# A two-layer encoder on one core: the last norm's scale row made on chip instead of through DRAM, and its finishing products placed wider apart

## The chip, the cores and the metric

The kernel runs on one core of one Trainium2 chip. The metric is the device time of one execution in microseconds (us). Three runs of the kernel before took 3623.66, 3624.28 and 3625.88 us; their median is 3624.28 us.

## The reference

The reference is an encoder trunk of two layers over 2048 tokens of 1024 features, in float32. Layer 0 mixes tokens by windowed attention, layer 1 by latent attention. Behind each mixer a gated input embedding is added, and behind the last layer stands one more norm. Only this ending matters here:

```python
for i in range(DEPTH):
    ...
    h = h + y
    gate = jax.nn.sigmoid(rms_norm(h, ple_norm_g[i]) @ ple_w_gate[i])
    h = h + (p[i] @ ple_w[i]) * gate
return rms_norm(h, final_norm_g)

def rms_norm(x, g):
    xf = x.astype(jnp.float32)
    y = xf * lax.rsqrt(jnp.mean(xf * xf, axis=-1, keepdims=True) + EPS)
    return (y * g.astype(jnp.float32)).astype(x.dtype)
```

So the last norm needs, for every token, one over the root of the mean square of its 1024 features, and it can be computed only when all 1024 features of `h` for that token are there.

## The kernel before

Activations lie in SBUF with features on the 128 partitions and tokens along the free dimension, so 1024 features are eight tiles, f = 0 to 7, and a reduction over features is a matmul with a matrix of ones. Each float32 product is made from three matmuls of split operands (`mm3`, L294 to L296), so one output tile of 128 features x 512 tokens takes 8 x 3 = 24 matmuls. Below, these 24 are called a product.

The end of the program is the second `Post` object (layer 1, `self.final`). Its back half goes over five token groups, `self.segs`: groups 0, 1 and 2 of 512 tokens, groups 3 and 4 of 256. For each group and each f:

- PE makes the gate product (`back`).
- `mixin` runs through the other engines: DVE takes the product out of PSUM and scales it (L926), ACT applies the sigmoid (L931), POOL multiplies by the embedding tile (L933), DVE adds to the residual `hf` (L935), ACT squares the new `hf` (L831).
- `gather` adds the square to the group's accumulator (L837, on POOL; for group 4 on DVE).
- The embedding tile comes from DRAM by `p_load` (L908, issued by SP) into a ring of two tiles, so load f + 2 can be issued only when POOL has used tile f.
- During groups 0 to 2 ACT and DVE also split the residual of a later group into matmul operands (`h_cut`, L232 and L233). The residual tiles of groups 3 and 4 are loaded (L891) into the same SBUF tiles that group 0 leaves free.

When all eight squares of a group are gathered, the scale row (1 / rms, for every token, on all 128 partitions) has to be made, and then `finish` (L944, DVE) multiplies each of the eight `hf` tiles by gain and row, and `h_store` (L940, SP) writes it out. There are two ways to the row:

- Groups 0 to 2 use `sums_at`: split the accumulator (ACT L220, DVE L222), two matmuls with ones (L270), copy one row to SBUF (L849), write it to DRAM (`sum_out`, L860), read it back with tokens on partitions (L866), take the root (L240, ACT L244, L248 to L253), write it to DRAM again (`root_out`, L880) and read it back spread over all partitions (`row_in`, L287).
- Groups 3 and 4 use `turn`, six steps on chip: one float32 matmul of ones with the accumulator (L954), DVE picks the diagonal of each 128 x 128 piece into a column (L960), root as above, PE transposes the broadcast column back (L974), ACT copies the row to SBUF (L978).

The order of the work on PE, DVE, ACT and POOL is written out by hand. `Plan.add(t, f, ...)` records a step with a planned time, the steps are sorted by it, and each engine runs its instructions strictly in that order. The times have meaning only for the order. One product is `UNIT` = 5.19 of them. The order of DMAs on SP is not set by the plan; a scheduler of the framework sets it, and SP too runs in order, so a DMA that waits holds up all behind it. `PS_SB` = 10 and `SUMS` place the steps of `sums_at` behind a group's end, `PL_SUM` those of `turn` for group 3.

Of the kernel before, what the change touches and what calls it, by code (L numbers as in the profile page):

```python
# [21 lines left out]
NC8 = D // P  # L22
TG = 512
# [12 lines left out]
PS_X, PS_EV, PS_ST, PS_SS, PS_H, PS_P, PS_HS, PS_SB = 4.4, 0.61, 2.06, 9.3, 1.2, 3, 0.68, 10  # L36
# [14 lines left out]
SUMS = (3, 4.2, 5, 7.5, 16.5, 16.7, 19, 20)  # L51
CUTAT, GATHB = (2.7, 1.9), 7.05
G_W, G_U = (-15.79, -9, 2, 8), -9.81
PL_SUM = (4.5, 5.8, 6.6, 8, 9.5, 10.6)
VLAG, GATHAT, ACCAT, DENAT, RECIPAT = 4.3, 1.3, 1.4, 8.4, 13.4
KLAG, RLAG, OLAG, DLAG, ILAG = 1, 0.8, 1, 0.8, 0.6
KAT = (6, 12)
# [78 lines left out]
class Plan:  # L136
# [5 lines left out]
    def add(self, t, f, *args):  # L142
        self.steps.append((t, f, args))
# [537 lines left out]
class Post:  # L681
# [329 lines left out]
    def schedule(self, plan, base, tables):  # L1011

        add = lambda t, f, *args: plan.add(base + t * US, f, *args)
        for t, f, args in tables:
            add(t, getattr(self, f), *args)
        add(5 if self.final else 0.3, self.spread_init)
        for tg in range(NG):
            for f in range(NC8):
                t = (NC8 * tg + f) * UNIT
                te = t + UNIT + PS_EV  # L1020
                add(t, self.front, tg, f)
                add(te - PS_X, self.x_load, tg, f)
                add(te, self.add, tg, f)
                add(te + 0.9, self.x_square, tg, f)
                add(te + 1.6, self.gather, 1, tg, f)
                add(te + PS_ST, self.x_store, tg, f)
                if tg > 0:
                    before = 3 + f // 2 if tg == 1 else NC8 * (tg - 1) + f
                    to = (3 + f / 2 if tg == 1 else before) * UNIT + 0.6
                    add(to - PS_OL2 - (6 if tg > 1 else 1.3), self.o_load, tg, f)  # L1030
                    add(before * UNIT - 0.01, self.o_spread, tg, f)
                    add(to, self.o_gate, tg, f, "both")
                    add(to + CUTAT[tg > 1], self.o_cut, tg, f, "both")
                    if f == 0:
                        add(to - 9, self.spread_load, tg)
                        add(to - 4.5, self.spread_cut, tg)
            self.sums_at(add, NC8 * (tg + 1) * UNIT + (PS_SS if tg < NG - 1 else 6.29), 1, tg)
        t = NG * NC8 * UNIT
        for tg in range(NG):
            tb = t + NC8 * tg * UNIT  # L1040
            add(tb - (PS_R1 if tg < NG - 1 else PS_R2), self.row_in, 1, tg)
            for f in range(NC8):
                th = tb - NC8 * UNIT + (0.5 + 0.8 * f if tg == 0 else 1.2 + 0.75 * f) * UNIT + PS_H
                add(th - PS_HL - (0 if tg == 0 else 2), self.h_load, tg, f)
                add(th, self.h_cut, tg, f)
        for g, (lo, n) in enumerate(self.segs):
            x, last = n / TG, self.final and g == len(self.segs) - 1
            unit = x * UNIT
            for f in range(NC8):
                te = t + unit + PS_EV  # L1050
                add(t, self.back, g, f)
                add(te - PS_P, self.p_load, g, f)
                for i, dt in enumerate((0, 0.9, 1.7, 3.2, 4.1) if n == TG else (0, 0.55, 1, 1.9, 2.5)):
                    add(te + dt, self.mixin, g, f, i)
                if last or g == len(self.segs) - 1 and f == NC8 - 1:
                    dt = 4.9 if n == TG else 3
                else:
                    dt = GATHB if n == TG else 3.7
                add(te + dt, self.gather, 2, g, f, "vector" if last else "gpsimd")
                t += unit  # L1060
                if not self.final:
                    add(te + 4.2 + PS_HS, self.h_store, g, f)
            if not self.final or n == TG:
                self.sums_at(add, t + (PS_SB if n * (g + 1) < T else PS_SL), 2, g)
            else:
                if last:
                    add(te + 0.6, self.warm_root)
                    for f in (2, 5):
                        add(te + 2.7, self.gain, g, f)
                times = [te + 3.1 + 0.01 * i for i in range(6)] if last else [te + dt for dt in PL_SUM]  # L1070
                for i in range(6):
                    add(times[i], self.turn, g, i)
                for f in range(NC8):
                    if last:
                        add(times[5] + 0.01 + 0.01 * f, self.finish_last, g, f)
                    else:
                        add(times[5] + 0.8 + f, self.finish, g, f)
                        add(times[5] + 1.6 + f, self.h_store, g, f)
            if self.final and n == TG:
                fin = t + PS_SB + 26  # L1080
                add(fin - 3, self.row_in, 2, g)
                for f in range(NC8):
                    add(fin + 1.3 * x * f, self.finish, g, f)
                    add(fin + 1.3 * x * f + 1, self.h_store, g, f)

    def enter(self, plan, base, early):

# [753 lines left out]
```

## Time and profile before

| | |
|---|---|
| median of three runs | 3624.28 us |
| the profiled execution | 3625.45 us |
| its span, first to last instruction | 3623.7 us |
| PE busy in the span | 3522.8 us (97%) |
| DVE, ACT, POOL busy | 2453.7, 2277.4, 1987.7 us |
| mean granted TensorE clock | 0.990 of 2.4 GHz |

The profiled execution is 1.75 us longer than its span, and 1.17 us longer than the median of the runs. All times of rows below are microseconds from the start of the span. A row of the timeline gives start, duration, engine, line, operation, and in brackets the idle time of the engine before it and what ended that.

### The profile page before, as it was taken

Reading aid. Unit: us, or ns where it says so; the run is one execution under the profiler, and the core shown is the slowest. Engines: PE = TensorE matmul, PEld = TensorE weight load, DVE = VectorE, ACT = ScalarE, POOL = GpSimd, SP = SyncE. Lnnn points to the kernel's source line nnn. Section 1 sums busy time; section 2 is a strip of 40 time slices with the busy share of each in tenths; the row PEclk is TensorE's granted clock in tenths of the full one; section 3 lists DMA queues with packets and bytes.
Section 4 is the critical chain, followed back from the end, with each engine's and each line's share of the span. In section 5 each row is a group of like instructions: output and inputs, shape, how many; then the busy total and the mean of one; then the engine's idle time right before and its main releaser. Section 6 shows DMA issues by size and latency. Waiting matters only on the chain.

```text
span 3623.7 us, 52443 instructions
## 1 busy us (share of the span) xinstructions
PE 3522.8 (97%) x17118; PEld 2949.7 (81%) x17118; DVE 2453.7 (68%) x4539; ACT 2277.4 (63%) x4268; POOL 1987.7 (55%) x1565
## 2 busy tenths in 40 slices
PE   7999999999999899999999999999999999989996
PEld 6888878877888889898888888888888888868876
DVE  6111169997456544425989898989898989985465
ACT  6211179995244533423889898989898989952332
POOL 5331210024334422113889898989898989964343
PEclk9999999999999999999999999999999999999998
DMA  5332388887655865834121212121212121066533
GB/s 187 136 122 90 94 208 202 201 201 225 190 147 150 195 223 185 267 122 107 43 54 42 52 31 53 33 58 36 59 35 57 34 68 36 20 195 205 164 96 105
DMA packets 380098, 428.19 MB, mean 118 GB/s; under 512 B 46303, under 2 KB 233183, under 8 KB 379118
## 3 DMA queue, kind: packets, MB, share of 16 engines
q1 hardware_dynamic: 360814, 390.75, 39.0%
q10 hardware_dynamic: 19008, 34.09, 2.5%
q8 instruction: 134, 2.20, 0.3%
q14 instruction: 142, 1.16, 0.1%
HBM read 251.65 MB, written 156.17 MB: 113 GB/s over the span
## 4 chain that ended last, share of the span: by engine, by line
PE 84%; DVE 6%; DMA 3%; ACT 2%; issue 2%; POOL 1%; SPq 0%; ACTq 0%; DVEq 0%; POOLq 0%
PE ps L296 13%; PE ps L294 13%; PE ps L295 13%; PE ps L1620 7%; PE ps L1653 6%; PE ps L1651 6%; PE ps L1683 6%; PE ps L1652 6%; PE ps L1684 6%; PE ps L601 2%; PE ps L615 1%; DVE blkF L935 1%; PE ps L557 1%; PE ps L556 1%; PE ps L616 1%
## 5 line engine op out<-in xcount | busy, mean ns | idle before, releaser
L1663 POOL TENSOR_TENSOR blkR<-blkF,blkX 128x512 fp32r<-128x512 f32 x1024 | 1352.0, 1332 | 179.3 <-PE ps L1653 51.7
L1624 DVE TENSOR_REDUCE blkF<-ps 128x1 f32<-128x512 f32 x1024 | 700.3, 684 | 79.4 <-PE ps L1620 43.7
L1655 ACT ACTIVATE blkF<-ps 128x512 f32<-128x512 f32 x1024 | 611.5, 597 | 100.6 <-PE ps L1653 57.2
L1656 ACT CAST blkX<-blkF 128x512 fp32r<-128x512 f32 x1024 | 635.5, 621 | 32.8
L1673 DVE TENSOR_TENSOR ps<-ps,blkF 128x512 f32<-128x512 f32 x896 | 615.3, 687 | 0.7
L1684 PE MATMUL ps<-blkR 128*128 128x512 f32 x1024 | 405.7, 396 | 1.1 <-POOL blkR L1663 1.1
L1683 PE MATMUL ps<-blkX,blkR 128*128 128x512 f32 x1024 | 405.7, 396 | 0.0
L294 PE MATMUL ps<-blkR 128*128 128x512 f32 (+2 forms) x888 | 337.7, 380 | 3.2 <-ACT blkR L220 2.8
L296 PE MATMUL ps<-blkR 128*128 128x512 f32 (+2 forms) x888 | 336.0, 378 | 0.5 <-DVE blkR L222 0.5
L295 PE MATMUL ps<-blkR 128*128 128x512 f32 (+2 forms) x888 | 335.6, 378 | 0.0
L367 DVE TENSOR_TENSOR blkF<-ps,blkF 128x512 f32<-128x512 f32 x72 | 49.5, 691 | 301.8 <-PE ps L296 292.1
L222 POOL TENSOR_TENSOR blkR<-blkF,blkR 128x512 fp32r<-128x512 f32 (+1 forms) x40 | 74.0, 1855 | 302.2 <-ACT blkR L220 274.9
L831 ACT ACTIVATE blkF<-blkF 128x512 f32<-128x512 f32 (+1 forms) x120 | 72.4, 603 | 261.2 <-DVE blkF L935 139.0
L1684 PEld LDWEIGHTS ps<-blkR 128*128 128x128 f32 x1024 | 195.0, 190 | 46.9 <-POOL blkR L1663 2.3
L1683 PEld LDWEIGHTS ps<-blkX,blkR 128*128 128x128 f32 x1024 | 195.0, 190 | 44.3
L837 POOL TENSOR_TENSOR blkF<-blkF 128x512 f32<-128x512 f32 (+1 forms) x112 | 159.5, 1424 | 99.3 <-ACT blkF L831 98.3
L933 POOL TENSOR_TENSOR blkF<-blkF 128x512 f32<-128x512 f32 (+1 forms) x70 | 85.8, 1225 | 223.2 <-ACT blkF L931 192.5
L294 PEld LDWEIGHTS ps<-blkR 128*128 128x128 f32 x888 | 168.0, 189 | 34.5 <-ACT blkR L220 3.1
L296 PEld LDWEIGHTS ps<-blkR 128*128 128x128 f32 x888 | 167.6, 189 | 31.6 <-DVE blkR L222 1.2
L295 PEld LDWEIGHTS ps<-blkR 128*128 128x128 f32 x888 | 167.9, 189 | 28.2
L227 DVE TENSOR_TENSOR blkR<-ps,blkR 128x512 fp32r<-128x512 f32 (+2 forms) x232 | 143.6, 625 | 47.5 <-ACT blkR L226 47.3
L1651 PE MATMUL ps<-blkZ 96*128 96x512 f32 x384 | 155.6, 405 | 6.8 <-ACT blkF L1655 6.8
(272 smaller groups left out, 9110.2 us busy)
## 6 DMA issues: line engine op xcount, KB each, us to landing
h<-blkF SPq DMA_DIRECT2D x96, 256.0 KB
blkF<-h SPq DMA_DIRECT2D x82, 256.0 KB
a_qs<-blkF ACTq DMA_DIRECT2D x64, 256.0 KB
ple<-blkF SPq DMA_DIRECT2D x64, 256.0 KB
b_v<-blkX SPq DMA_DIRECT2D x32, 512.0 KB
b_q<-blkX SPq DMA_DIRECT2D x64, 256.0 KB
blkZ<-b_q SPq DMA_DIRECT2D x64, 256.0 KB
blkF<-h SPq DMA_DIRECT2D x31, 512.0 KB
```

The lines of the kernel that those rows point to most:

```text
L294: mm(out, lhsT=lh, rhs=rh, start=(first and i == 0), stop=False)
L295: mm(out, lhsT=lh, rhs=rl, start=False, stop=False)
L296: mm(out, lhsT=ll, rhs=rh, start=False, stop=(last and i == n - 1))
L1620: nc.tensor.matmul(ps, lhsT=qh[0:96, qt * P : (qt + 1) * P], rhs=self.kh[h % 3][0:96, kc * TG : (kc + 1) * TG], start=True, stop=True,)
L1624: nc.vector.tensor_reduce(out=mm[:, qt, kc : kc + 1], in_=ps, axis=AX.X, op=ALU.max)
L1651: nc.tensor.matmul(sp, lhsT=kl[:, kt_], rhs=qh[0:96, :], start=True, stop=False)
L1655: nc.scalar.activation(pe, sp, AF.Exp, scale=SCALE_B)
L1656: nc.scalar.copy(ph, pe)
L1663: nc.gpsimd.tensor_tensor(out=pl, in0=pe, in1=fv(ph), op=ALU.subtract)
L1673: nc.vector.tensor_tensor(out=st["acc"], in0=prev, in1=st[kt][0], op=ALU.add)
L1683: nc.tensor.matmul(st["o"], lhsT=v, rhs=ph, start=(kt == 0), stop=False)
L1684: nc.tensor.matmul(st["o"], lhsT=v, rhs=pl, start=False, stop=(kt == NT - 1))
```

## The change

Groups 0 to 2 make their row by `turn` like groups 3 and 4, with planned times `PT_TURN` behind the group's end; nothing of them goes by DRAM any more. `sums_at` and `row_in` for the last norm are gone. The eight `finish` steps of a full group follow the row at a distance of 2.3 each, where it was 1.3, and they start at about 22.6 behind the group's end (19.9 for group 2), where it was 36. `PL_SUM` of group 3 is later by 2.3 to 2.8, and its `finish` steps are 0.85 apart, where it was 1. In the changed kernel all lines of the functions concerned have numbers larger by one.

```diff
-PL_SUM = (4.5, 5.8, 6.6, 8, 9.5, 10.6)
+PL_SUM = (7.1, 8.4, 8.9, 11, 12.3, 13)
+PT_TURN = ((10.37, 11.8, 12.4, 14.5, 20.75, 21.6), (10.37, 11.8, 12.4, 14.5, 18.15, 18.9))
...
-            if not self.final or n == TG:
+            if not self.final:
                 self.sums_at(add, t + (PS_SB if n * (g + 1) < T else PS_SL), 2, g)
+            elif n == TG:
+                times = PT_TURN[g == 2]
+                for i, dt in enumerate(times):
+                    add(t + dt, self.turn, g, i)
+                for f in range(NC8):
+                    add(t + times[5] + 1 + 2.3 * f, self.finish, g, f)
+                    add(t + times[5] + 2 + 2.3 * f, self.h_store, g, f)
...
-                        add(times[5] + 0.8 + f, self.finish, g, f)
-                        add(times[5] + 1.6 + f, self.h_store, g, f)
-            if self.final and n == TG:
-                fin = t + PS_SB + 26
-                add(fin - 3, self.row_in, 2, g)
-                for f in range(NC8):
-                    add(fin + 1.3 * x * f, self.finish, g, f)
-                    add(fin + 1.3 * x * f + 1, self.h_store, g, f)
+                        add(times[5] + 0.8 + 0.85 * f, self.finish, g, f)
+                        add(times[5] + 1.6 + 0.85 * f, self.h_store, g, f)
```

On PE the two matmuls of L270 stood behind the third product of the next group (the sixth, for the half products of group 3). Now one float32 matmul of 512 columns stands behind the second (the fourth) product, and four transposes stand behind the fourth (the seventh). The matmul for group 3's row moves from behind the second product of group 4 to behind the third.

On SP, this is the stretch of groups 3 and 4 in the kernel before, where group 2's row goes out and comes back (`rs`); `ple` rows are the embedding loads, `out` rows the stores.

```order
L908 DMA blkF<-ple_84 128x256
L866 DMA blkF<-sq_92 128x4x1
L908 DMA blkF<-ple_84 128x256 x4
L880 DMA rs_97<-blkF 128x4x1
L287 DMA blkF<-rs_97 128x512
L908 DMA blkF<-ple_84 128x256
L940 DMA out<-blkF 128x256
```

The same stretch on SP in the changed kernel:

```order
L909 DMA blkF<-ple_84 128x256 x9
L941 DMA out<-blkZ 128x512 x2
L909 DMA blkF<-ple_84 128x256
L941 DMA out<-blkZ 128x512
L909 DMA blkF<-ple_84 128x256
```

The write of `rs`, and the read that waits for it, no longer stand ahead of the loads for group 4; stores of group 2 stand between these loads instead of behind them.

On SP in group 1, in the changed kernel, `out` rows are the stores of group 0 and `h_86` rows reload its tiles for groups 3 and 4:

```order
L941 DMA out<-blkF 128x512
L892 DMA blkF<-h_86 128x512 x2
L909 DMA blkF<-ple_84 128x512
L941 DMA out<-blkF 128x512 x2
L892 DMA blkF<-h_86 128x512 x2
L941 DMA out<-blkF 128x512 x2
L909 DMA blkF<-ple_84 128x512
L892 DMA blkF<-h_86 128x512
```

Before, all eight stores of group 0 were due at the end of group 1, with the loads of `rs` ahead of them; now the stores and the reloads alternate with the embedding loads through the second half of group 1.

On DVE, this is the end of group 1 in the kernel before: L926 takes a product out of PSUM, L935 adds, L944 is a finishing product of group 0.

```order
L926 TENSOR_TENSOR blkF<-ps,blkF 128x512
L233 SCALAR_TENSOR_TENSOR blkR<-blkZ,gam,blkR 128x512
L935 TENSOR_TENSOR blkZ<-blkZ,blkF 128x512
L944 SCALAR_TENSOR_TENSOR blkF<-blkF,gam 128x512
L926 TENSOR_TENSOR blkF<-ps,blkF 128x512
L944 SCALAR_TENSOR_TENSOR blkF<-blkF,gam 128x512 x3
L935 TENSOR_TENSOR blkZ<-blkZ,blkF 128x512
```

The finishing products of group 0 in the changed kernel:

```order
L927 TENSOR_TENSOR blkF<-ps,blkF 128x512
L945 SCALAR_TENSOR_TENSOR blkF<-blkF,gam 128x512
L234 SCALAR_TENSOR_TENSOR blkR<-blkZ,gam,blkR 128x512
L936 TENSOR_TENSOR blkZ<-blkZ,blkF 128x512
L945 SCALAR_TENSOR_TENSOR blkF<-blkF,gam 128x512
L927 TENSOR_TENSOR blkF<-ps,blkF 128x512
L234 SCALAR_TENSOR_TENSOR blkR<-blkZ,gam,blkR 128x512
L945 SCALAR_TENSOR_TENSOR blkF<-blkF,gam 128x512 x2
```

They stood four between two takings-out in the last products of the group; now there are about two, from the fourth product (f = 3) on.

## Rows read from the trace of the kernel before

**Rows 1.** Busy time by window, PE only; PEclk is the granted clock.

```profile
core 0: us, PE busy (x), PEclk, DMA share, GB/s
3508.20:3513.40 5.20, 5.20 (x12) 0.50 0.68 241
3562.40:3568.30 5.90, 5.85 (x24) 0.50 0.17 47
```

**Rows 2.** Timeline of PE, groups 1 to 4: start, us, engine, line, operation, [idle before].

```profile
3458.51 0.62 PE L270 MATMUL ps<-blkE,ones 128*128 128x512 f32 x2
3458.97 0.40 PE L294 MATMUL ps<-blkR 128*128 128x512 f32 x1
...
3508.20 1.52 PE L270 MATMUL ps<-blkE,ones 128*128 128x512 f32 x2 [5.52 <-ACT blkE L220]
...
3562.38 1.63 PE L270 MATMUL ps<-blkE,ones 128*128 128x512 f32 x2 [6.22 <-ACT blkE L220]
...
3579.44 0.70 PE L954 MATMUL ps<-blkF,ones 128*128 128x256 f32 x2 [1.98 <-POOL blkF L837]
3579.79 0.47 PE L294 MATMUL ps<-blkR 128*128 128x256 f32 x1
...
3586.78 0.43 PE L974 MATMUL ps<-ident,blkF 128*128 128x128 f32 x2 [0.90 <-DVE blkF L253]
3586.97 0.36 PE L294 MATMUL ps<-blkR 128*128 128x256 f32 x1
...
3612.18 1.22 PE L954 MATMUL ps<-blkF,ones 128*128 128x256 f32 x2 [13.45 <-DVE blkF L837]
```

**Rows 3.** Chain of work that ended last, in order of time: start, us, what.

```profile
3498.21 4.90 DMA out<-blkF
...
3530.19 14.04 DMA blkF<-ple
...
3585.56 8.59 DMA rs<-blkF
...
3594.58 5.27 DMA blkF<-ple
3599.98 0.87 POOL blkF L933
```

**Rows 4.** Timeline of DVE: ends of groups 0 and 1, a pick, the last product.

```profile
3440.44 0.68 DVE L926 TENSOR_TENSOR blkF<-ps,blkF 128x512 f32<-128x512 f32 x1
...
3444.86 0.68 DVE L926 TENSOR_TENSOR blkF<-ps,blkF 128x512 f32<-128x512 f32 x1
...
3490.10 0.75 DVE L944 SCALAR_TENSOR_TENSOR blkF<-blkF,gam 128x512 f32<-128x512 f32 x1 [3.77 <-DMA blkF<-rs]
3490.77 0.68 DVE L926 TENSOR_TENSOR blkF<-ps,blkF 128x512 f32<-128x512 f32 x1
...
3496.76 0.68 DVE L926 TENSOR_TENSOR blkF<-ps,blkF 128x512 f32<-128x512 f32 x1
...
3580.29 0.29 DVE L960 CUSTOM_DVE_ANT_0 blkF<-ps,ident 128x128 f32<-128x128 f32 x1 [0.21 <-PE ps L954]
...
3580.62 0.29 DVE L960 CUSTOM_DVE_ANT_0 blkF<-ps,ident 128x128 f32<-128x128 f32 x1
...
3608.39 0.41 DVE L926 TENSOR_TENSOR blkF<-ps,blkF 128x256 f32<-128x256 f32 x1
```

**Rows 5.** Timeline of POOL: the last gathering of groups 0, 1 and 2.

```profile
3451.97 1.74 POOL L837 TENSOR_TENSOR blkF<-blkF 128x512 f32<-128x512 f32 x1
...
3504.72 1.71 POOL L837 TENSOR_TENSOR blkF<-blkF 128x512 f32<-128x512 f32 x1
...
3559.49 1.26 POOL L837 TENSOR_TENSOR blkF<-blkF 128x512 f32<-128x512 f32 x1
```

**Rows 6.** Timeline of ACT: a change of tables in group 1.

```profile
3472.16 1.28 ACT L244 ACT_TABLE_LOAD   x1
3473.46 0.20 ACT L244 ACTIVATE blkF<-blkF 128x4 f32<-128x4 f32 x1
```

## Prediction, made before the changed kernel was run

> **What bounds the kernel now.** I read the page first: PE is busy for 97% of the span (the table above), so a change can win little but PE's pauses. The page's slices show where the change works: PE and its clock fall off in the last two of forty. I then read PE's timeline there, the chain of waits, and the timelines of DVE, POOL and SP.
>
> From group 1 on PE pauses five times [rows 2]: 5.52 us before the sum matmul of group 1, 6.22 before that of group 2, 1.98 and 0.90 before the matmul and the transposes of group 3, and 13.45 between the last product and the last sum. The first two cost twice, for the granted clock is 0.50 (1.2 GHz) for 5.2 and 5.9 us behind them [rows 1]: half of that, 5.55 us, is lost again.
>
> The reader is to see that the same thing is behind the largest of them. The row of group 2 goes out to DRAM, and the write takes 8.59 us to land; the read of it and, behind that in SP's queue, the embedding loads of group 4 wait for it, and the next load lands only 5.27 us later, when POOL can go on [rows 3]. POOL, DVE and ACT stand still meanwhile and PE, which works ahead, has nothing left to do. In group 1 it is DVE that stands still, 3.77 us at a finishing product whose row is not back [rows 4]. From there DVE does not catch up: two takings-out lie 4.42 us apart at the end of group 0 (3440.44 to 3444.86) but 5.99 at the end of group 1, where four finishing products lie between them [rows 4]. So the last gathering is late, and PE stands in order behind it.
>
> How late is a number that I need below. L270 of group 0 started at 3458.51 without a wait, behind three products; two matmuls take 0.46 there, so a product of 24 takes about 5.5 us, and group 0's last product ended near 3442.2. Its last gathering ended at 3453.71, 11.5 behind it [rows 2, 5]. For group 1 the last product ended near 3486.3 (3502.68 less three products) and the gathering at 3506.43, 20.1 behind; for group 2 the last product near 3539.0 (3556.16 less six half products) and the gathering at 3560.75, 21.7 behind [rows 2, 5].
>
> **The change, part by part.**
>
> *New work on PE.* A float32 sum matmul of 256 columns holds PE for 0.35 us (3579.44 to 3579.79), so one of 512 about 0.70; it replaces the pair of L270 with 0.46. Two transposes hold it for 0.19, four for 0.38 [rows 2]. That is 0.62 per group, 1.9 us for three, all on the path since PE is the bound here. The Trainium skill, "FP8 and Floating Point Precision", TensorE Precision Notes, says that true float32 takes four passes; by that rule 512 columns would take four times 0.23, some 0.9, and the sum would be 0.6 us larger. The row has 0.35 for 256 and decides.
>
> *The round trip goes.* With it go three waits of SP, and what is queued behind them comes on time. The four pauses before the last product come to 5.52 + 6.22 + 1.98 + 0.90 = 14.62 us, and the slow clock to 5.55. I take all of it away and put the new waits in separately.
>
> *The sum matmul moves forward.* It stands one product earlier than L270, 11 us behind a group's end instead of 16.5, and PE waits there for the last gathering, with all later products queued behind it. ACT's and DVE's splitting drops out, so only the gathering counts. At group 0 it is 11.5 behind: 0.5 to 0.7 us of wait, new. At groups 1 and 2 it depends on whether the lag falls from 20.1 and 21.7 to group 0's 11.5. Lower bound: nothing. Upper bound: the lag stays, 9.1 and 10.7 us.
>
> *DVE.* It loses the wait of 3.77 us, and the finishing products stand two between takings-out instead of four. Four of them raised the interval by 1.57, 0.39 each; eight in a group make 3.1 us if none finds a gap, and PE's 5.5 per product leaves 1.1 over DVE's 4.42 to make up for it. The four picks of a group are new, at 0.33 each (3580.29 to 3580.62), 1.3 us [rows 4]; they come at the third product, where five products follow to catch up. So I expect a lag between 11.5 and 14.6 and take 1.4 us of wait for each of groups 1 and 2, nearer the lower end since most finishing products find DVE waiting for POOL. With group 0's 0.7 that is 3.5 us.
>
> *ACT.* The changes of tables for the root are as many as before, but for group 2 they fall at half products. A load takes 1.28 us and the next operation starts 1.30 behind it [rows 6]. The Trainium skill, "ScalarE: Activation LUTs", What ACT_TABLE_LOAD costs, adds a drain of about 1380 ns, 2.66 us for each change; by that rule group 2's two changes would add 2.7 us of lag where there is little to make it up, and the time would be 3603. The rows show no such drain, so I count nothing more; what cover is lost is in the lag above.
>
> *The end.* Without the wait for the embedding load PE's last pause is the natural one, from the last product through DVE, ACT, DVE's multiply, add, square and gathering. From the last L926 at 3608.39 to the sum matmul at 3612.18 this took 3.79 us [rows 2, 4]. With 0.6 for a remaining lag I take 4.4 instead of 13.45, 9.05 less. Bounds: 3.8, and 3.8 + 3.1 if all finishing products of groups 2 and 3 add to the lag.
>
> *SP.* Stores of group 0 and the reloads into the same tiles now alternate with embedding loads in group 1. A reload waits until the store of its tile has landed, 4.90 us [rows 3]; three embedding loads stand behind such reloads, and each is needed about two products after it could be issued. I count nothing; the last rival prices it.
>
> *Sum.* -14.6 - 5.55 + 1.9 + 3.5 - 9.05 = -23.8 us against the profiled execution of 3625.45. The median of the runs lies 1.17 us below that one, so the forecast is 3625.45 - 23.8 - 1.17 = 3600.5 us. With no new waits at all and no lag at the end it would be 3.5 + 0.6 lower, 3596.4.
>
> **Rivals.**
>
> *The waits come back at the new place.* DVE and POOL share the work as tightly as before, the lag at groups 1 and 2 stays near 16 to 17, and PE waits at the earlier sum matmul about as long as it did at L270, 11.7 us with the slow clock of 5.55 behind it. For it: DVE's interval of 5.99 at the end of group 1 is over PE's 5.5 [rows 4]. Against it: group 0, without finishing products, has 11.5. The new waits are then 17.3 instead of 3.5: 3600.5 + 13.8 = 3614.3 us.
>
> *The lag doesn't fall at all.* Then PE waits 9.1 and 10.7 us instead of 5.52 and 6.22, because it comes to the matmul a product earlier. Waits of 0.7 + 19.8 and a slow clock of 5.55 stand in place of 3.5: 3600.5 + 22.5 = 3623 us, no change, since only the end and the pauses of group 3 are won. For it: if the lag came from the changes of tables, which stay. Against it: DVE's row names the DMA.
>
> *SP becomes the bound; slower.* The reloads of group 0's tiles stand ahead of the embedding loads of group 1's last products and group 2's first. The third of these can be issued only after three store landings in series, behind the second store. With 4.90 us each, 15 us, it comes in time; with landings of L it is late by about 3 L - 20. Slower than now by more than 7 us takes 31 us over the forecast, with 2.7 of them the slow clock behind one such pause, so it decides from L = 16; at L = 17 the time is 3600.5 + 31 + 2.7 = 3634 us. For it: one DMA of the chain took 14.04 us [rows 3]. Against it: the stores are spread wider, so fewer are in flight together.
>
> **Chances and range.** About 0.2%, 7 us, is what a measurement of this kernel can tell from no change; so under 3617.0 is faster and over 3631.5 slower. Forecast 0.66, waits at the new place 0.19, lag unchanged 0.11, SP 0.04. The forecast's own range is 3595 to 3608, from no new waits to the upper ends of the lag (3.6 for each of two groups, 3.1 at the end). The range for eight in ten goes on to the first rival: 3594 to 3614. All of the forecast and about nine in ten of the first rival are faster: 0.83; the rest of that and the unchanged lag are within: 0.13; SP is slower: 0.04.
>
> **What would show it.** Right: no pause of PE over 2 us between the start of group 1 and the last product, the clock at 1.00 there, the last product ended near 3579 to 3584 where it was 3598.7, a last pause of 4 to 5 us, and last gatherings 11 to 14 us behind the end of their groups. Wrong: a pause of 5 us or more at the float32 sum of group 1 or 2 (first and second rival, told apart by the lag of the gathering), POOL waiting for an embedding load with SP's queue at a reload (third), or a last pause still near 13 us, which would mean that the load was not what held POOL.

## The result and the profile after

The changed kernel takes 3597.97 us (median of four runs, 3595.71 to 3599.66) against 3625.08 beside it; the ratio is 0.992, with a 95% interval of 0.9905 to 0.9935. The forecast was 3600.5, with a range of 3594 to 3614. The profiled execution took 3595.71 us, with a span of 3593.7. Below, TensorE is PE of the rows, VectorE is DVE, ScalarE ACT, GpSimd POOL and SyncE SP.

About 3 us of the difference between the two spans arose ahead of the groups that were changed. The last sum of the front norm, which both kernels have, started 3 us earlier:

Before, TensorE's timeline at that sum (start, duration in us, engine, line, operation; a wait stands in brackets):

```profile
3409.04 0.39 PE L270 MATMUL ps<-blkE,ones 128*128 128x512 f32 x1
```

After, the same instruction, and then all sum matmuls behind it, with the last transposes:

```profile
3406.03 0.39 PE L271 MATMUL ps<-blkE,ones 128*128 128x512 f32 x1
...
3452.58 1.13 PE L955 MATMUL ps<-blkF,ones 128*128 128x512 f32 x2 [2.36 <-POOL blkF L838]
3497.56 1.02 PE L955 MATMUL ps<-blkF,ones 128*128 128x512 f32 x2
3543.06 1.02 PE L955 MATMUL ps<-blkF,ones 128*128 128x512 f32 x2
3564.48 0.59 PE L955 MATMUL ps<-blkF,ones 128*128 128x256 f32 x2
3582.91 0.70 PE L955 MATMUL ps<-blkF,ones 128*128 128x256 f32 x2 [3.25 <-DVE blkF L838]
3585.76 0.69 PE L975 MATMUL ps<-ident,blkF 128*128 128x128 f32 x2 [2.16 <-DVE blkF L254]
```

From that sum to the end of the span it is 214.7 us before (3623.7 - 3409.04) and 187.7 after, 27.0 less. I use this stretch below, since what runs ahead of it varies by more than most experiments are worth: in the profiles of this study the sum started anywhere from 3406 to 3417 us.

The reader is to compare with [rows 2]. The pauses of 5.52, 6.22, 1.98 and 0.90 us are gone; one of 2.36 is new, at group 0's sum; the last one fell from 13.45 to 3.25. The clock is not lowered behind the sums of groups 0 to 3 (columns: stretch, its length, busy time of PE, granted clock, DMA share, GB/s), where [rows 1] have 0.50:

```profile
3452.60:3458.00 5.40, 5.40 (x22) 1.00 0.15 44
3497.60:3503.00 5.40, 5.40 (x24) 1.00 0.30 97
3543.10:3548.50 5.40, 5.40 (x42) 1.00 0.17 52
3564.50:3568.00 3.50, 3.50 (x30) 1.00 0.49 171
```

The last gatherings of groups 1 and 2 on GpSimd, and VectorE at the first finishing product of group 0 and of group 2, which answer to [rows 4, 5]:

```profile
3495.50 1.73 POOL L838 TENSOR_TENSOR blkF<-blkF 128x512 f32<-128x512 f32 x1
...
3540.41 1.30 POOL L838 TENSOR_TENSOR blkF<-blkF 128x512 f32<-128x512 f32 x1
```
```profile
3465.70 0.75 DVE L945 SCALAR_TENSOR_TENSOR blkF<-blkF,gam 128x512 f32<-128x512 f32 x1 [0.29 <-ACT blkF L979]
...
3554.79 0.75 DVE L945 SCALAR_TENSOR_TENSOR blkZ<-blkZ,gam,blkF 128x512 f32<-128x512 f32 x1 [0.62 <-ACT blkF L979]
```

Where these two groups end on TensorE is seen from the next group's first product:

```profile
3486.67 0.39 PE L295 MATMUL ps<-blkR,blkX 128*128 128x512 f32 x1
...
3531.54 0.28 PE L295 MATMUL ps<-blkR,blkX 128*128 128x256 f32 x1
```

So the gatherings, at 3497.23 and 3541.71, end 10.6 and 10.2 us behind their groups; before it was 20.1 and 21.7. The first finishing product of groups 0 and 1 waits 0.29 us for its row, that of group 2 0.62 us.

### The profile page after: what moved, and what is told of

It reads as the page before. It is cut to its first block, busy times and chain, and to the rows that moved or that the text cites. A ratio compares the mean times of both kernels' runs of the same rounds, so it can differ in the third digit from the quotient of the medians.

```text
span 3593.7 us, 52467 instructions
## 1 busy us (share of the span) xinstructions
PE 3519.4 (98%) x17130; PEld 2948.9 (82%) x17130; DVE 2455.7 (68%) x4560; ACT 2275.5 (63%) x4265; POOL 1983.9 (55%) x1565
## 4 chain that ended last, share of the span: by engine, by line
PE 82%; DVE 5%; DMA 5%; ACT 2%; issue 2%; POOL 1%; SPq 1%; ACTq 0%; DVEq 0%; POOLq 0%
PE ps L297 12%; PE ps L295 12%; PE ps L296 12%; PE ps L1622 7%; PE ps L1655 6%; PE ps L1653 6%; PE ps L1685 6%; PE ps L1654 6%; PE ps L1686 6%; DMA h<-blkF 3%; PE ps L602 2%; PE ps L617 1%; PE ps L616 1%; PE ps L557 1%; PE ps L558 1%
```

## Experiments

The times of before in the four sets of runs were 3625.1, 3631.5, 3630.2 and 3629.6 us, so only ratios are compared. The last column is the stretch from the last front sum to the end of the span, in one profiled execution.

| kernel | ratio to before, 95% interval | stretch, us |
|---|---|---|
| before | | 214.7 |
| changed | 0.9920 [0.9905, 0.9935] | 187.7 |
| changed, again | 0.9921 [0.9908, 0.9935] | 185.5 |
| E1 new way for group 2 alone | 0.9962 [0.9947, 0.9977] | 205.3 |
| E2 new way for groups 0 and 1 | 0.9953 [0.9938, 0.9968] | 198.9 |
| E3 changed, late close finish | 0.9924 [0.9909, 0.9939] | 190.9 |
| E4 before, loads ahead | 1.0013 [1.0003, 1.0023] | 215.1 |
| E5 changed, early close finish | 0.9916 [0.9900, 0.9933] | 189.4 |
| E6 changed, group 0's sum later | 0.9913 [0.9900, 0.9927] | 186.6 |
| E7 E6, table load later | 0.9913 [0.9900, 0.9927] | 187.1 |
| E8 before, spread finish | 0.9996 [0.9986, 1.0005] | 216.8 |
| E9 before, late finish | 1.0000 [0.9991, 1.0009] | 217.4 |
| E10 E9 with loads ahead | 0.9999 [0.9990, 1.0009] | 209.5 |

### E1 and E2: which row makes which pause

```
-            if not self.final:
+            if not self.final or g in OLD:        # E1: OLD = (0, 1); E2: OLD = (2,)
                 self.sums_at(...)
...
+            if self.final and n == TG and g in OLD:   # row_in, finish and store as before
```

E2 also has group 3's old times.

E1: 

> The new way for group 2 alone; groups 0 and 1 keep the way by DRAM with their finish at the old place, group 3 has the new times. My theory (each pause belongs to the row of the group before it): TensorE's pauses of 5.52 and 6.22 us at the sums of groups 1 and 2 stay within 1.5 us, with the low clock behind them; those at group 3's sum and transpose (1.98, 0.90) go and the last one falls from 13.45 to 3 to 5 us; 2.9 + 10 - 0.6 = about 12.3 us gained, 3612 to 3614 us. Rival 1 (the three rows disturb each other, one left by DRAM is enough for an end pause): last pause above 8 us, 3617 or more. Rival 2 (the pauses at the sums come from the finish of any row at the end of the next group, not from one row each): pause at group 2's sum below 3 us, 3608 or less.

E2: 

> The other half: the new way for groups 0 and 1, group 2 by DRAM as before, group 3 with its old times. My theory: no pause above 1 us at the sums of groups 1 and 2 and clock 1.00 there, 11.74 + 5.55 us back, less the 2.36 us pause at group 0's sum and 1.2 us of new TensorE work, 13.7 us gained: 3611 to 3613 us; the last pause stays at 12 to 14 us and group 3's two pauses (1.98, 0.90) stay. The gains of this kernel and of the one with group 2 alone then add up to the whole 27 us within 2 us. Rival (what arrives earlier is waited for at the end: lost time moves behind group 3): last pause above 16 us, 3617 us or more.

TensorE's sums in E1, from group 1 on, and then in E2, from group 0 on:

```profile
3507.05 1.52 PE L272 MATMUL ps<-blkE,ones 128*128 128x512 f32 x2 [5.45 <-ACT blkE L222]
3560.18 2.07 PE L956 MATMUL ps<-blkF,ones 128*128 128x512 f32 x2 [10.64 <-POOL blkF L839]
3583.61 0.59 PE L956 MATMUL ps<-blkF,ones 128*128 128x256 f32 x2
3602.04 1.22 PE L956 MATMUL ps<-blkF,ones 128*128 128x256 f32 x2 [3.24 <-DVE blkF L839]
```
```profile
3461.11 1.12 PE L956 MATMUL ps<-blkF,ones 128*128 128x512 f32 x2 [1.92 <-POOL blkF L839]
3506.11 1.02 PE L956 MATMUL ps<-blkF,ones 128*128 128x512 f32 x2
3557.37 0.63 PE L272 MATMUL ps<-blkE,ones 128*128 128x512 f32 x2
3569.35 0.59 PE L956 MATMUL ps<-blkF,ones 128*128 128x256 f32 x2
3602.96 1.22 PE L956 MATMUL ps<-blkF,ones 128*128 128x256 f32 x2 [14.48 <-DVE blkF L839]
```

The large pauses go with the rows, as my theory had it. With the rows of groups 0 and 1 by DRAM, the sums of groups 1 and 2 wait; with group 2's, the last sum waits 14.48 us. Which of the first two rows holds group 2's sum, these two kernels do not separate, since they keep or drop both; in E1's trace VectorE waits 6.53 us for group 1's row, until 3544.28, ahead of that sum. One expectation failed: in E2 the pause of 1.98 us at group 3's sum, which was to stay with group 2's row, is gone, so that row alone does not make it (0.86 us at the transposes stayed). The 10.64 us in E1 was not expected either. Group 2's sum stands two half products earlier there, and group 1's row still holds the gatherings: this is close to the price of 10.7 us that the prediction worked out for a lag that stays. By the stretch the two halves gain 9.3 and 15.8 us, 25.1 together against the whole 27.0; by the ratios about 14 and 17.

### E4, E9 and E10: what held the last sum

The prediction blamed the embedding load that stands behind the row's write and read in SyncE's queue. In the same trace VectorE waits 7.03 us for the row itself. Both waits in the kernel before, and above them VectorE's wait for the row of group 1:

```profile
3544.84 0.75 DVE L944 SCALAR_TENSOR_TENSOR blkZ<-blkZ,gam,blkF 128x512 f32<-128x512 f32 x1 [5.94 <-DMA blkF<-rs]
...
3599.50 0.75 DVE L944 SCALAR_TENSOR_TENSOR blkZ<-blkZ,gam,blkF 128x512 f32<-128x512 f32 x1 [7.03 <-DMA blkF<-rs]
```
```profile
3599.98 0.86 POOL L933 TENSOR_TENSOR blkF<-blkF 128x256 f32<-128x256 f32 x1 [9.82 <-DMA blkF<-ple]
```

These kernels take away the one, the other, and both, in the kernel before.

```
 E4, E10: eight tiles of 256 columns for groups 3 and 4, loads earlier
+    early = unit * (4 if g == 4 else 2 if g == 3 and f > 1 else 0)
-    add(te - PS_P, self.p_load, g, f)
+    add(te - PS_P - early, self.p_load, g, f)
 E9, E10: a third tile for the rows, and
-    add(fin + 1.3 * x * f, self.finish, g, f)
+    add(fin + (0, 10, 14)[g] + 1.3 * f, self.finish, g, f)
```

E4 and E10 put the embedding blocks of the last 512 tokens into other tiles and don't keep the reference's values there; the instructions and transfers are as many and as large, so waits and times can be read from them. In both, four of the loads for the last groups went out before the last front sum already (from 3394.90 in E4, from 3400.16 in E10), among the front norm's own transfers; the order on SyncE is not the plan's.

E4: 

> The kernel before, with eight tiles for the embedding blocks of groups 3 and 4 and their loads up to four products earlier, so that all of them stand ahead of the write and the read of group 2's row in SyncE's queue; nothing else. The reason given in the prediction (GpSimd waits 9.82 us for an embedding load that stands behind the row's write): GpSimd's wait goes and the last pause falls from 13.45 to 4 to 6 us, 3615 to 3617 us. Rival (VectorE stands in its own queue at the first finishing product until the row itself has landed, 7.03 us in the trace before, and the last blocks' taking-out, last in VectorE's queue, is held by that): GpSimd's wait goes, VectorE's wait for the row stays at 6 us or more and the last pause at 10 to 13 us, 3622 to 3626 us.

E9: 

> The kernel before, rows by DRAM as they were, but the finishing products of group 1 planned 10 us later and those of group 2 14 us later, behind everything else of VectorE; a third tile for the rows; embedding loads as before. My theory now (a row's wait costs only by what stands behind the first finishing product in VectorE's queue): the pause at group 1's sum (row of group 0, not moved) stays at 5 to 7 us, that at group 2's sum falls from 6.2 to below 1.5 us; at the end VectorE's wait goes, GpSimd's wait for the embedding load stays at 8 to 11 us and keeps the last pause at 9 to 12 us; 11 to 14 us gained. Rival 1 (GpSimd's load is no cause at all): last pause 3 to 6 us, 16 us gained or more. Rival 2 (the way by DRAM itself slows the rest, by its sum, splits and table load): the pause at group 2's sum stays above 3 us, 6 us gained or less.

E10: 

> The same with the embedding loads of groups 3 and 4 ahead of group 2's row in SyncE's queue as well, in eight tiles. With the load moved alone the last pause was 12.55 us. My theory (two waits beside each other, for the row on VectorE and for the load on GpSimd, each long enough to hold the end): with both gone the last pause is 3 to 6 us; eight finishing products of 0.7 us and their stores then come behind the last block's, 5 to 6 us on the end; 12 to 17 us gained on the kernel before. Rival (a third wait, that for the slow gatherings of the last blocks, holds the end): last pause above 8 us, 10 us gained or less.

E4: GpSimd at the multiply that had waited 9.82 us for its load and at the next one, VectorE at the first finishing product of group 2, and TensorE's last sum:

```profile
3596.78 0.80 POOL L934 TENSOR_TENSOR blkF<-blkF 128x256 f32<-128x256 f32 x1 [1.72 <-ACT blkF L932]
3606.55 1.05 POOL L934 TENSOR_TENSOR blkF<-blkF 128x256 f32<-128x256 f32 x1 [8.97 <-ACT blkF L932]
```
```profile
3604.21 0.75 DVE L945 SCALAR_TENSOR_TENSOR blkZ<-blkZ,gam,blkF 128x512 f32<-128x512 f32 x1 [6.35 <-DMA blkF<-rs]
```
```profile
3616.18 1.22 PE L955 MATMUL ps<-blkF,ones 128*128 128x256 f32 x2 [12.55 <-DVE blkF L838]
```

GpSimd no longer waits for a load. It does one more block, and then stands for 8.97 us behind ScalarE, which waits for VectorE's taking-out, which stands behind the finishing product that waits for the row. The last pause fell by 0.9 us only: the expectation from the prediction's reason failed, and its rival came.

E9: GpSimd's two waits for loads, and TensorE's sums of groups 2 and 4:

```profile
3548.56 1.29 POOL L933 TENSOR_TENSOR blkF<-blkF 128x512 f32<-128x512 f32 x1 [6.37 <-DMA blkF<-ple]
...
3603.05 0.72 POOL L933 TENSOR_TENSOR blkF<-blkF 128x256 f32<-128x256 f32 x1 [10.66 <-DMA blkF<-ple]
```
```profile
3563.34 0.50 PE L270 MATMUL ps<-blkE,ones 128*128 128x512 f32 x1 [3.76 <-ACT blkE L220]
...
3612.11 1.22 PE L954 MATMUL ps<-blkF,ones 128*128 128x256 f32 x2 [10.79 <-DVE blkF L837]
```

VectorE waits for neither of the two moved rows now, and nothing is won. At the end the load takes over as expected (10.79 us). At group 2's sum I had expected less than 1.5 us; 3.76 remain. Group 1's row has a load behind it too: GpSimd waits 6.37 us for it, where before VectorE's own wait of 5.94 us lay. That this load makes the 3.76 us is read from the trace, not shown: no kernel takes it away (E10 does not move the loads of group 2), and the signs of rival 2, above 3 us there and 6 us gained or less, came as well. What that rival names can be seen in part in the kernel before: between the last gathering and the sum, where ScalarE splits the accumulator, lie 1.77 us in group 1 (3506.43 to 3508.20) and 1.63 in group 2. What the sums of groups 2 and 4 wait less, 2.1 and 2.7 us, is spent again: 1.3 us more at group 1's sum, 2.0 more at group 3's, and 5.4 more behind the last sum, where the eight finishing products now stand (16.89 us where it was 11.52).

E10: TensorE's sums of groups 2, 3 and 4, and VectorE's last instructions:

```profile
3568.75 0.50 PE L270 MATMUL ps<-blkE,ones 128*128 128x512 f32 x1 [3.51 <-ACT blkE L220]
3587.12 1.22 PE L955 MATMUL ps<-blkF,ones 128*128 128x256 f32 x2 [4.03 <-POOL blkF L837]
3609.97 0.70 PE L955 MATMUL ps<-blkF,ones 128*128 128x256 f32 x2 [3.25 <-DVE blkF L837]
```
```profile
3616.31 5.38 DVE L945 SCALAR_TENSOR_TENSOR blkZ<-blkZ,gam,blkF 128x512 f32<-128x512 f32 x8
```

With both gone the last pause is 3.25 us, the same as in the changed kernel. (Not all of the 10.2 us need be the waits: E9 and E10 also take eight finishing products from among the last blocks, and E3 below, whose row is made on chip, has 2.8 us more with them there.) So the end of the kernel before had two waits side by side, each nearly long enough by itself: taking away one leaves 12.55 or 10.79 of 13.45, and both together leave 3.25. The finishing products then have to come behind the last block, 5.38 us. The stretch is 5.1 us shorter than before, less than the 12 to 17 I expected: the pauses ahead of the last product come to 15.3 us (7.42 at group 1's sum, 3.51 and 0.34 at group 2's, 4.03 at group 3's), no less than the 14.62 of before, and the tail is 4.9 us longer. The median shows no gain at all. Why it shows none is open: in the profiled execution the last front sum came at 3416.87, later than in any other. The four early loads among the front's transfers are a candidate that no run tests.

### E8, E3 and E5: the place and the spacing of the finishing products

```
 E8: before, groups 0 and 1 spread
-    add(fin + 1.3 * x * f, self.finish, g, f)
+    add(fin + (1.3 if g == 2 else 2.3) * f, self.finish, g, f)
 E3: changed, old start and spacing           E5: changed, spacing 1.3
-    add(t + times[5] + 1 + 2.3 * f, ...      -    add(t + times[5] + 1 + 2.3 * f, ...
+    add(t + PS_SB + 26 + 1.3 * f, ...        +    add(t + times[5] + 1 + 1.3 * f, ...
```

E8: 

> The kernel before, with the finishing products of groups 0 and 1 2.3 us apart in the plan and not 1.3, at the same start; rows still by DRAM, group 2's finish as before. My theory (of the 5.5 and 6.2 us pauses at the next sums some part is VectorE's wait for the row, 3.8 us, and some the four finishing products of 0.75 us that stand between two takings-out): pauses of 3 to 4 us remain, 3618 to 3622 us. Rival 1 (the wait for the row alone does it): pauses stay at 5 to 6 us, 3624 to 3627 us. Rival 2 (the crowding alone does it): pauses below 1.5 us and clock 1.00, 3608 to 3612 us.

E3: 

> The changed kernel with the finishing products of groups 0 to 2 back at the start and the spacing of before (36 us behind the group, 1.3 us apart); the rows are made on chip as in the change. My theory (the wait for the row is what cost time, not where the products stand): no wait for a row, pauses at the sums of groups 1 and 2 below 1.5 us, last pause 3 to 6 us, since group 2's eight products of 0.75 us stand among the last takings-out; a gain of 22 to 27 us on the kernel before. Rival (start and spacing are half of the gain: eight products between the takings-out delay the gatherings by themselves): pauses of 2 to 4 us at the sums and 7 us or more at the end, a gain of 16 us or less.

E5: 

> The changed kernel with the finishing products at its early start but 1.3 us apart as before. My theory: nothing that TensorE waits for depends on it, the same time as the changed kernel within 1.5 us (25.5 to 28.5 us less than before), pauses as in it. Rival (the wider spacing carries part of the gain): new pauses of 1 us or more at sums, 24 us gained or less.

E8, VectorE at the first finishing product of group 0 and TensorE's sums of groups 1 and 2; then the last sum of E3, and that of E5:

```profile
3494.11 0.75 DVE L944 SCALAR_TENSOR_TENSOR blkF<-blkF,gam 128x512 f32<-128x512 f32 x1 [3.71 <-DMA blkF<-rs]
```
```profile
3511.47 1.52 PE L270 MATMUL ps<-blkE,ones 128*128 128x512 f32 x2 [6.40 <-ACT blkE L220]
3565.52 1.64 PE L270 MATMUL ps<-blkE,ones 128*128 128x512 f32 x2 [7.11 <-ACT blkE L220]
```
```profile
3590.68 1.22 PE L955 MATMUL ps<-blkF,ones 128*128 128x256 f32 x2 [6.05 <-DVE blkF L838]
```
```profile
3586.96 1.22 PE L955 MATMUL ps<-blkF,ones 128*128 128x256 f32 x2 [3.49 <-DVE blkF L838]
```

In E8 the pauses are 0.9 us longer than in [rows 2], but group 0's row also came later. The table has, from the last front sum on, when VectorE goes on with the row, and the pause at group 1's sum, for all kernels in which that row goes by DRAM:

| kernel | VectorE goes on, us | pause, us | difference |
|---|---|---|---|
| before | 81.06 | 5.52 | 75.54 |
| E1 | 81.00 | 5.45 | 75.55 |
| E4 | 82.34 | 6.78 | 75.56 |
| E9 | 82.39 | 6.84 | 75.55 |
| E10 | 83.00 | 7.42 | 75.58 |
| E8, spread | 82.69 | 6.40 | 76.29 |

In the five with the old spacing the pause follows the row one for one: a row that is a microsecond later makes the pause a microsecond longer. At E8's time they would have 7.1 us; E8 has 6.4, so spreading took 0.7 us off, about a tenth. My theory, that half of the pause was crowding, falls, and rival 1 (the wait for the row) holds but for this tenth. At group 2's sum no such relief can be read. In the other direction, with rows made on chip, the products may stand nearly as close as before: E3 and E5 keep 23.8 and 25.3 us of the 27.0. At group 1's sum E3, close at the old place, has a pause of 0.70 us, which again says how little the crowding costs without the wait. What E3 loses is mostly at the end, a pause of 6.05 us instead of 3.25, since group 2's eight products lie among the last takings-out. E5 has small new pauses, 0.23 us at group 1's sum and 0.90 at group 3's transposes, and its ratio is no worse than the changed kernel's; its 1.7 us are within what two executions of one kernel differ.

### E6 and E7: two attempts to do better

```
 E6: PT_TURN for group 0: (10.37, 11.8, ...) -> (15.56, 17, 17.6, 19.7, 25.94, 26.8)
 E7: E6, and
-    add(te + 0.6, self.warm_root)
+    add(te + 2.51, self.warm_root)
```

The changed kernel again: 

> The changed kernel once more, as the measure for the two kernels beside it: 26 to 31 us less than the kernel before, a pause of 2.36 us at group 0's sum and 3.25 us at the last sum, 187.7 us from the last front sum to the end of the span.

E6: 

> The changed kernel with group 0's sum, root and transposes one product (5.19 us) later in the plan. My theory (group 0's sum is asked for before its last gathering is done, and that is the one new wait of the change): no pause above 0.3 us there, 2.2 to 2.6 us less from the last front sum to the end of the span (185.1 to 185.5 us); by the median 1 to 4 us less than the changed kernel, at the edge of what the runs can tell. Rival (TensorE's pause is made up later, since the gatherings set the pace up to the end): the pause goes, another one of 1 us or more appears at a later sum or the last one grows, less than 1 us gained.

E7: 

> The same, and the early load of the root's table (at the end) moved behind the last block's square. My theory (the table load, 1.28 us on ScalarE, stands before the last square and delays it by 0.5 us, and the end pause by as much): last pause 2.6 to 2.9 us, 0.4 to 0.6 us less from the last front sum to the end of the span than the kernel with the later sum alone. Rival (the load then stands before the last root, which waits for it): last pause 2.7 us, but the wait between the last sum and the last transposes grows from 2.16 us by 0.3 us or more, and nothing is gained.

Sums on TensorE: of group 0 and the last one in the changed kernel's second profile, of groups 0 and 1 in E6, and of group 1 and the last one in E7:

```profile
3459.53 1.02 PE L955 MATMUL ps<-blkF,ones 128*128 128x512 f32 x2
...
3589.76 1.22 PE L955 MATMUL ps<-blkF,ones 128*128 128x256 f32 x2 [3.25 <-DVE blkF L838]
```
```profile
3456.75 1.02 PE L955 MATMUL ps<-blkF,ones 128*128 128x512 f32 x2
3497.48 1.13 PE L955 MATMUL ps<-blkF,ones 128*128 128x512 f32 x2 [1.14 <-POOL blkF L838]
```
```profile
3503.37 1.13 PE L955 MATMUL ps<-blkF,ones 128*128 128x512 f32 x2 [1.53 <-POOL blkF L838]
...
3588.46 1.22 PE L955 MATMUL ps<-blkF,ones 128*128 128x256 f32 x2 [2.85 <-DVE blkF L838]
```

My expectation for the second execution failed: the 2.36 us at group 0's sum are not there, though the program is the same, and the stretch is 2.2 us shorter. GpSimd's first multiply of group 0 in the first execution, and in the second:

```profile
3407.07 1.29 POOL L934 TENSOR_TENSOR blkF<-blkF 128x512 f32<-128x512 f32 x1 [4.31 <-DMA blkF<-ple]
```
```profile
3412.66 1.28 POOL L934 TENSOR_TENSOR blkF<-blkF 128x512 f32<-128x512 f32 x1 [3.29 <-ACT blkR L233]
```

In the first it waits for an embedding load and starts 1.0 us behind the last front sum; in the second it waits for ScalarE and starts 2.9 us ahead of it. Most of this stays: the fifth multiply came at 3429.37, 23.3 us behind the last front sum, in the first execution, and 20.1 behind in the second. So that pause varies between executions, and in these two with a load's landing. With the sum moved there is none at group 0, but one of 1.14 us at group 1 in E6 and of 1.53 in E7, which has the same edit: the rival's picture, in both profiles. E7 takes 0.40 us off the last pause, as expected; its stretch, expected to be 0.4 to 0.6 us shorter than E6's, is 0.5 longer, so this is lost in the variation of the rest. Neither beats the changed kernel by its ratio.

## Why the prediction was right, step by step

The forecast was a gain of 23.8 us on the profiled execution; the stretch gives 27.0 in the first profile and 29.2 in the second.

- **The pauses and the slow clock, 14.62 + 5.55.** Right: all gone [rows 1, 2]. E2 shows that the two at the sums of groups 1 and 2 hung on the rows of groups 0 and 1, and the table under E8 that the first follows its row one for one.
- **New work on PE, 1.9.** Read too low. The sum of group 1 in the changed kernel, and what stands behind it:

```profile
3497.56 1.02 PE L955 MATMUL ps<-blkF,ones 128*128 128x512 f32 x2
3498.02 0.80 PE L295 MATMUL ps<-blkR 128*128 128x512 f32 x1
3498.65 0.40 PE L296 MATMUL ps<-blkR 128*128 128x512 f32 x1
```

  The next matmul starts after 0.46 us, but the one behind it only 0.63 later, where matmuls of 512 columns follow each other at 0.23. So the sum costs 1.09 less 0.23, 0.86 us. The prediction took the distance to the next start alone, 0.35 us for 256 columns, so 0.70; the figure of some 0.9 that it set aside fits better. Four transposes cost 0.44 us by the same reading (3509.32 to 3509.99 less 0.23), so that a group has 0.84 us more and three have 2.5. Over the stretch this does not show by itself: up to the end of the last product 16.06 us were won, and 20.17 less the new pause of 2.36 less 16.06 leaves 1.8 for all else, the new work and what the other terms are off by.
- **New waits, 3.5 (0.7, 1.4, 1.4).** Mis-sized, and in the wrong place: 2.36, 0 and 0 in the first profile, none in the second. The forecast let the finishing products and the picks lengthen the lag to between 11.5 and 14.6 us; it went to 10.6 and 10.2. Most finishing products find VectorE idle between GpSimd's results: in E5, at 1.3 us, group 1's sum waits 0.23 us only.
- **The end, 9.05.** Mis-sized by 1.15: the pause is 3.25, below the 3.8 taken as lowest. The 3.79 us read for the natural pause had three finishing products of group 2 in it (L944 at 3608.72, 3610.05 and 3611.05); without them the same way takes 3.21 (3579.70 to 3582.91). But the reason given was half of the truth. The prediction named the embedding load behind the row's write; E4 takes that away, and the last pause falls by 0.9 us. VectorE's wait for the row is the other half, 7.03 us in the trace before; the prediction leaves it out, and the chain of waits [rows 3] that it goes by runs through GpSimd. The forecast of the end came out because the change removes the row's trip, and so both waits; this much of it was luck.
- **The cause of the lag in group 1.** The prediction split it between a wait of 3.77 us and four finishing products between takings-out [rows 4]. E8 spreads these products and takes off 0.7 of 7.1 us, and E3, which keeps them close at the old place but has the row on chip, pauses 0.70 us at that sum; the rest goes with the wait.
- **ScalarE's tables.** In the tail the load of the root's table takes 1.28 us and the next operation starts 1.30 behind its start, as in [rows 6]:

```profile
3580.59 1.28 ACT L1001 ACT_TABLE_LOAD   x1
3581.89 0.20 ACT L1001 ACTIVATE blkF<-ident 128x1 f32<-128x1 f32 x1
```

  The drain that the Trainium skill, "ScalarE: Activation LUTs", What ACT_TABLE_LOAD costs, adds to it is not seen here. One load stands on the path at the end and adds 0.4 us to the last pause (3.25 against 2.85 in E7).
- **The rivals.** The waits didn't come back at the new place (pauses 0 at groups 1 and 2). E1 shows the second rival's price in the one place where its condition holds: 10.64 us, worked out as 10.7. Two signs of being right were missed on the good side: a last pause of 4 to 5 us and a lag of 11 to 14. SyncE did not become the bound: no wait of GpSimd for an embedding load at the reloads.
- **Not in the forecast:** the tail behind the last sum is 10.79 us in the first profile and 11.24 in the second against 11.52 before (3623.7 - 3612.18). The last sum took 0.70 us in the first and 1.22 in the second and before, with equal pauses of 3.25 in the two; this 0.5 us is not the change's. In the first profile most misses go one way: the end, the new waits and the tail gave 1.2, 1.1 and 0.7 us more than forecast, the new work 0.6 less; 0.8 of the 3.2 us between 23.8 and 27.0 stay unassigned.

## What to carry to other kernels

A chain of waits names one of the engines that stand still at the same time; before blaming its transfer, look for a second wait of the same length on another engine, since taking away one of two may buy little (0.9 or 2.7 us of 10). A result that comes back by DRAM costs what stands behind its reader, in the reader's queue and in the queue that issues it, so three rows of 2 KB cost 27 us; made on chip, they free the place of the products that use them. Compare executions from a common instruction shortly ahead of the change, when what runs before it varies more than the edit is worth; and where a wait hangs on a landing, compare at the same landing, or a real gain (0.7 us in E8) hides behind a later one.

## What the runs showed of the hardware

- An equal pause of 3.25 us ahead of the last sum left that matmul at 0.70 us in one execution and at 1.22 in another of the same program; behind pauses of 6.05 and 3.49 us (E3, E5) it took 1.22.
- A float32 sum matmul of 512 columns held back what stood behind it by 0.86 us at a granted clock of 1.00, though the next matmul started after 0.46: the price is seen at the second start behind it.
- Executions of one program differ by several us ahead of the changed groups (the last front sum at 3406.03 and 3415.51 in two profiles of the changed kernel), and by about 2 us in the last 190 us.
